# A macaron decoder layer: the mixer run for all 512 tokens at once, its weights split beforehand into DRAM, and one channel group of the long convolution on ScalarE and GpSimd

## The chip, the cores and the metric

The kernel runs on one core of one Trainium2 chip. The time is device microseconds of one execution. PE is TensorE (PEld its weight loads), DVE is VectorE, ACT is ScalarE, POOL is GpSimd, SP is SyncE, which issues most of the DMAs. The span runs from the first to the last instruction of one profiled execution.

## The reference

One layer on x of 512 tokens by 1024, in float32: two half-step SwiGLU FFNs around a token mixer, each behind an RMS norm.

```python
x = x + 0.5 * swiglu(rmsnorm(x, ffn1_norm))          # 1024 -> 2816 -> 1024
h = rmsnorm(x, mix_norm)
c_val, c_gate, r_x, r_gate = split(h @ w_in, 4)      # 512 channels each
u = c_val * sigmoid(c_gate)
u = silu(layernorm(causal_depthwise_conv(u, 31 taps) + bias))
xr = causal_depthwise_conv(r_x, 4 taps) + bias
r = sigmoid(block_diag(xr, w_a) + b_a); i = sigmoid(block_diag(xr, w_x) + b_x)
a = exp(-8 * r * softplus(-lam))
y = scan(h_t = a_t * h_(t-1) + sqrt(1 - a_t^2) * i * xr) * gelu(r_gate)
x = x + concat(u, y) @ w_out                         # 1024 -> 1024
x = x + 0.5 * swiglu(rmsnorm(x, ffn2_norm))
out = rmsnorm(x, final_norm)
```

## The kernel before, in words

**Split products.** Every large product is made of three: a float32 operand is written as hi + lo, hi being the value cast to float32r and lo the difference, and hi*hi, hi*lo and lo*hi are accumulated in PSUM. Weights come in slabs of 128x1024. A slab is loaded by SP into one of 3 `raw` buffers, cast by ACT (L127) and subtracted by DVE or, where a unit is marked shared, by POOL (L141) into one of 5 `hl` buffers. A slab gives 24 matmuls of 512 columns (or 24 of 256 for half of the tokens).

**The list of units.** The kernel is a list `u` of units (L692 on), each one slab's matmuls with what follows them. `run` (L167) walks the list, issues loads, casts and subtractions 5, 3 and 2 slabs ahead, and after each unit steps `chains` (norms, LRU, LayerNorm: generators whose pieces are put between units) and `convs` (single convolution taps, as long as a planner's estimate of DVE's clock lies behind that of PE). A scheduler then orders each engine's instructions once and for all, by priority and by its own estimate of when each is ready; `tc.high_priority(offset=...)` moves a chain's priority, and a higher-priority instruction that isn't ready is passed by others. On the chip each engine follows its fixed order.

**The stages.** First FFN: 22 feature tiles of gate and up, the first 10 with their down projection (`down_a`), the other 12, then `down_b`. `down_b` is run for tokens 0 to 255, then for 256 to 511, because each token block needs two PSUM banks and four are at hand (`pd`; four more are `pp`). Everything from there to the ninth feature tile of the second FFN is done in two halves of 256 tokens, so that one half's chains run beside the other half's matmuls: w_in's 16 slabs are loaded and split twice, as are w_out's 8 and ten of the 12 of `down_b`, and nine FFN2 tiles run as A and, later, B.

**The mixer's chains.** `conv31` (L503) makes 31 taps for each of four channel groups on DVE, `acc = ub * w + acc`, on 128x256 with `acc` in PSUM. `layernorm` (L534) adds the four groups on DVE, averages over channels with a matmul against a matrix of 1/512 (`channel_mean`, L523), subtracts, squares, averages again, and makes u's hi and lo. `rx_units` (L458) evacuate r_x and run the four-tap convolution on DVE with SBUF operands only (L472). `lru` (L568) makes the gates with small float32 matmuls on PE (L577), sigmoid, tanh, exp and square root on ACT, two products on POOL (L581, L600), the scan (L605) and the product with the gelu gate on DVE, then y's hi and lo. `out_units` (L414) waits for u and y of one half. The norms (`norm_chain`, L264) take a square on ACT, two tiny POOL instructions, a scale on DVE (L235), transposes on PE (L251) and an evacuation into `h_hi` and `h_lo`.

Of the kernel before, what the change touches and what calls it, by code (L numbers as in the profile page):

```python
# [21 lines left out]
NG = 7  # L22
NG2A = 9
ND = 4
# [5 lines left out]
POOL_CUT = 1  # L30
POOL_AHEAD = 1.0
DVE_AHEAD = 0.0
NY1 = 0
NY2 = 1
NY3 = 0
NY4 = 0
KEEP = 2
NARROW = 16
PIN_T = True
PIN_A = False  # L40
PR_NORM = 800
PR_CONV = -50
PR_LRU0 = 0
PR_LRU1 = 0
PR_LN = 200
G_ZC = True
G_Y0 = True
YF0 = False
YF1 = True
ORDER = 0  # L50
PR_FIRST = 50
RMS_EPS = 1e-6
LN_EPS = 1e-5

(P_DW, P_DWB, P_LNG, P_LNB, P_LW, P_LCB, P_BA, P_BX, P_LAM, P_N) = (
    0, 31, 32, 33, 34, 38, 39, 40, 41, 42)


@with_exitstack
def layer_kernel(ctx: ExitStack, tc, x, gains, w_g1, w_u1, w_d1a, w_d1b, w_in,  # L60
# [7 lines left out]
    pd = ctx.enter_context(tc.tile_pool(name="pd", bufs=4, space=bass.MemoryType.PSUM))  # L68
    pp = ctx.enter_context(tc.tile_pool(name="pp", bufs=4, space=bass.MemoryType.PSUM))
# [7 lines left out]
    def const(shape, name, dt=F32):  # L77
        return cp.tile(shape, dt, name=name, tag=name)

# [14 lines left out]
    hlast = const([P, 4], "hlast")  # L94
# [11 lines left out]

    clock = {"pe": 0.0, "dve": 0.0, "pool": 0.0}
    chains, convs, done = [], [], {}
# [3 lines left out]


    class Narrow:
        def __init__(self, ap):
            self.ap = ap


    def slab_load(st, src):
        st["raw"] = wp.tile([P, D], F32, name=nm("raw"), tag="raw", bufs=RAW_BUFS)  # L120
        nc.sync.dma_start(st["raw"], src)

    def slab_hi(st, narrow):
        hl = wp.tile([P, 2 * D + 64], F32R, name=nm("hl"), tag="hl", bufs=HL_BUFS)
        o = NARROW if narrow else 0
        st["hl"] = hl[:, o:o + 2 * D].rearrange("p (s d) -> p s d", s=2)
        S.copy(st["hl"][:, 0, :], st["raw"])  # L127

    def slab_lo(st, shared):
        eng = V  # L130
        if shared:
            clock["pool"] = max(clock["pool"], clock["pe"])
            if clock["pool"] - clock["pe"] < POOL_AHEAD:
                eng = G
                clock["pool"] += 2.4
        if eng is V:
            dve(1.15)
        n = POOL_CUT if eng is G else 1
        for i in range(n):
            sl = slice(i * D // n, (i + 1) * D // n)  # L140
            eng.tensor_sub(st["hl"][:, 1, sl], st["raw"][:, sl],  # L141
                           st["hl"][:, 0, sl].bitcast(F32))
# [24 lines left out]
    def run(units, held):  # L167
# [4 lines left out]
        for i, (src, shared, us, mm, evac) in enumerate(x[:5] for x in units):  # L172
# [21 lines left out]
            if evac is not None:  # L194
                evac()
# [644 lines left out]
```

## Time and profile before

| | |
|---|---|
| runs | 936.29, 937.52, 939.07 us; median 937.52 |
| profiled execution | 936.05 us, its span 934.3 us, granted clock 0.982 |
| PE busy | 896.5 us of the span, 96% |
| DVE, ACT, POOL busy | 473.4, 368.7, 211.6 us |
| DMA | 115.94 MB, mean 124 GB/s; nearly all loads issued by SP, 512 KB each |

How to read the rows of the views: a row of the timeline gives start, duration, engine, line, operation, output<-inputs, shapes and count, and in brackets the idle time before it with what ended it. A row of the chain of waits gives start, the share of time on the chain and the instruction. A row of the groups gives line, engine, operation, tiles, shapes, count, then busy time and mean nanoseconds of one, then idle time before the group and what ended it. Overlapping instructions of one engine are merged, so a row's time can be shorter than count by mean.

### The profile page before, as it was taken

Reading aid. Unit: us, or ns where it says so; the run is one execution under the profiler, and the core shown is the slowest. Engines: PE = TensorE matmul, PEld = TensorE weight load, DVE = VectorE, ACT = ScalarE, POOL = GpSimd, SP = SyncE. Lnnn points to the kernel's source line nnn. Section 1 sums busy time; section 2 is a strip of 40 time slices with the busy share of each in tenths; the row PEclk is TensorE's granted clock in tenths of the full one; section 3 lists DMA queues with packets and bytes.
Section 4 is the critical chain, followed back from the end, with each engine's and each line's share of the span. In section 5 each row is a group of like instructions: output and inputs, shape, how many; then the busy total and the mean of one; then the engine's idle time right before and its main releaser. Section 6 shows DMA issues by size and latency. Waiting matters only on the chain.

```text
span 934.3 us, 11886 instructions
## 1 busy us (share of the span) xinstructions
PE 896.5 (96%) x4796; PEld 775.7 (83%) x4796; DVE 473.4 (51%) x677; ACT 368.7 (39%) x502; POOL 211.6 (23%) x120
## 2 busy tenths in 40 slices
PE   8999999999999999979889798999999999999997
PEld 6988888888888889879868797799988888888885
DVE  6533333333333433999999897455523333333224
ACT  6522321222232344357876644644421232223113
POOL 2000000000000058884756895700000000000001
PEclk9999999999999999998989898999999999999999
DMA  7323223222322445553433454455532322232202
GB/s 269 130 93 111 90 91 112 91 91 93 110 91 94 155 135 180 182 186 108 141 132 132 137 186 154 136 169 192 182 113 91 109 94 91 94 110 90 93 21 90
DMA packets 33401, 115.94 MB, mean 124 GB/s; under 512 B 4673, under 2 KB 4801, under 8 KB 33346
## 3 DMA queue, kind: packets, MB, share of 16 engines
q1 hardware_dynamic: 32770, 114.14, 36.9%
q10 hardware_dynamic: 576, 1.05, 0.3%
q8 instruction: 37, 0.61, 0.3%
q14 instruction: 18, 0.15, 0.1%
HBM read 113.07 MB, written 2.10 MB: 123 GB/s over the span
## 4 chain that ended last, share of the span: by engine, by line
PE 83%; DVE 12%; DMA 2%; ACT 1%; issue 1%; POOL 1%; SPq 0%; POOLq 0%; ACTq 0%; DVEq 0%
PE pgate L203 24%; PE pup L203 24%; PE pd L341 8%; PE pd L339 8%; PE pd L340 8%; PE pz L203 6%; DVE pc L516 4%; DVE xr L472 2%; PE pdl L341 1%; PE pdl L340 1%; PE pdl L339 1%; PE ptr L251 1%; DVE xn L235 1%; DMA raw<-in_w_u 1%; POOL hl L141 1%
## 5 line engine op out<-in xcount | busy, mean ns | idle before, releaser
L127 ACT CAST hl<-raw 128x1024 fp32r<-128x1024 f32 x208 | 217.8, 1048 | 327.5 <-PE pup L203 141.6
L141 DVE TENSOR_TENSOR hl<-raw,hl 128x1024 fp32r<-128x1024 f32 x136 | 168.1, 1237 | 283.9 <-ACT hl L127 283.9
L141 POOL TENSOR_TENSOR hl<-raw,hl 128x1024 fp32r<-128x1024 f32 x72 | 181.6, 2530 | 382.7 <-ACT hl L127 381.6
L203 PE MATMUL pup<-h_hi,hl 128*128 128x512 f32 (+1 forms) x880 | 179.7, 346 | 1.1 <-DVE sg L312 1.1
L203 PE MATMUL pgate<-h_hi,hl 128*128 128x512 f32 (+1 forms) x880 | 180.0, 347 | 0.7 <-ACT h_hi L255 0.7
L203 PEld LDWEIGHTS pgate<-h_hi,hl 128*128 128x128 f32 x880 | 144.2, 190 | 21.9 <-ACT h_hi L255 1.4
L203 PEld LDWEIGHTS pup<-h_hi,hl 128*128 128x128 f32 x880 | 144.1, 189 | 21.9 <-DVE sg L312 1.3
L339 PE MATMUL pd<-hl,act 128*128 128x512 f32 x304 | 118.5, 390 | 0.0
L340 PE MATMUL pd<-hl,act 128*128 128x512 f32 x304 | 118.3, 389 | 0.0
L341 PE MATMUL pd<-hl,act 128*128 128x512 f32 x304 | 118.3, 389 | 0.0
L516 DVE SCALAR_TENSOR_TENSOR pc<-ub,ch,pc 128x256 f32<-128x256 f32 x232 | 94.7, 478 | 0.0
L203 PE MATMUL pgate<-h_lo,hl 128*128 128x512 f32 (+1 forms) x440 | 89.8, 346 | 0.0
L203 PE MATMUL pup<-h_lo,hl 128*128 128x512 f32 (+1 forms) x440 | 89.3, 345 | 0.0
L298 ACT ACTIVATE sg<-pgate 128x512 f32<-128x512 f32 (+1 forms) x55 | 28.2, 513 | 151.2 <-PE pgate L203 151.2
L203 PEld LDWEIGHTS pgate<-h_lo,hl 128*128 128x128 f32 x440 | 72.0, 189 | 10.3
L203 PEld LDWEIGHTS pup<-h_lo,hl 128*128 128x128 f32 x440 | 71.7, 188 | 10.2
L312 DVE TENSOR_TENSOR sg<-pup,sg 128x512 f32<-128x512 f32 (+1 forms) x55 | 32.1, 583 | 87.9 <-PE pup L203 87.9
L768 POOL TENSOR_SCALAR sf<-sf 128x1 f32<-128x1 f32 x4 | 1.2, 302 | 319.1 <-ACT sqo L765 319.1
L203 PE MATMUL pz<-h_hi,hl 128*128 128x256 f32 x512 | 70.0, 287 | 0.1
L341 PEld LDWEIGHTS pd<-hl,act 128*128 128x128 f32 x304 | 57.1, 188 | 11.8
L340 PEld LDWEIGHTS pd<-hl,act 128*128 128x128 f32 x304 | 57.1, 188 | 11.8
L339 PEld LDWEIGHTS pd<-hl,act 128*128 128x128 f32 x304 | 57.1, 188 | 11.6
(118 smaller groups left out, 764.7 us busy)
## 6 DMA issues: line engine op xcount, KB each, us to landing
raw<-in_w_g SPq DMA_DIRECT2D x53, 512.0 KB, 3.3
raw<-in_w_u SPq DMA_DIRECT2D x53, 512.0 KB, 3.3
raw<-in_w_in SPq DMA_DIRECT2D x32, 512.0 KB, 3.4
raw<-in_w_d1b SPq DMA_DIRECT2D x22, 512.0 KB, 3.3
raw<-in_w_out SPq DMA_DIRECT2D x16, 512.0 KB, 3.3
raw<-in_w_d2b SPq DMA_DIRECT2D x12, 512.0 KB, 3.2
raw<-in_w_d1a SPq DMA_DIRECT2D x10, 512.0 KB, 3.3
raw<-in_w_d2a SPq DMA_DIRECT2D x10, 512.0 KB, 3.3
```

Of the source, the lines that this page charges most:

```text
L127: S.copy(st["hl"][:, 0, :], st["raw"])
L141: eng.tensor_sub(st["hl"][:, 1, sl], st["raw"][:, sl], st["hl"][:, 0, sl].bitcast(F32))
L203: PE.matmul(ps, w[:, a, k, :], h[:, k, t0:t0 + n], start=(s == 0 and k == 0), stop=(s == 2 and k == KT - 1))
L235: V.scalar_tensor_tensor(out=xn, in0=xt[t], scalar=ss[:, 1:2], in1=g, op0=ALU.mult, op1=ALU.mult)
L251: ins = PE.transpose(pt[:, k, :], xs[0][:, (hf * 4 + k) * P:(hf * 4 + k + 1) * P], ident)
L298: S.activation(sg[:, :n], pg[:, :n], AF.Silu)
L312: V.tensor_mul(sg[:, :n], pu[:, :n], sg[:, :n])
L339: PE.matmul(ps, ahi, whi, start=first, stop=False)
L340: PE.matmul(ps, ahi, wlo, start=False, stop=False)
L341: PE.matmul(ps, alo, whi, start=False, stop=last)
L472: V.scalar_tensor_tensor(out=xr[:, c, :], in0=rxb[:, c, half * HT + k:half * HT + k + HT], scalar=par(c, P_LW + k), in1=xr[:, c, :], op0=A ...
L516: V.scalar_tensor_tensor(out=cv[:, c, :] if j == 30 else acc, in0=src, scalar=par(c, P_DW + j), in1=acc, op0=ALU.mult, op1=ALU.add)
```

## The change

- **One pass.** The mixer runs for all 512 tokens: each w_in and w_out slab is used once. `down_b` runs its first 8 slabs for all four token blocks (8 PSUM banks, now one pool `pb`), and holds its last 4 slabs for two passes of two blocks each. The first two channel groups of the gated convolution input still run as halves A and B; so do the first two feature tiles of both FFNs; all else in FFN2 runs on 512 tokens.
- **Split beforehand.** `split_ahead` loads each of the 24 mixer slabs during the first FFN, casts it on ACT, subtracts on DVE and stores hi and lo to DRAM by DMAs issued on POOL. In the mixer a slab is one 1 MB load straight into `hl` (three of w_out's into six slots of the `act` tag). POOL makes no subtractions any more, in FFN2 either.
- **Convolution.** Three channel groups run on DVE with 31 taps of 128x512 each; the first one has its products made by ACT and its sums, two taps at a time, by POOL.
- **Around it.** The channel sums are four accumulating float32 matmuls instead of DVE sums and one matmul. The four-tap convolution accumulates in PSUM. `hlast` is gone. The output projection makes y's part for token blocks 0 to 2, then, behind the variance, for block 3, then u's part for all four; the norm before FFN2 is started by single token blocks. The yields that held one half's chains behind the other's are gone.

```diff
-    pd = ctx.enter_context(tc.tile_pool(name="pd", bufs=4, space=bass.MemoryType.PSUM))
-    pp = ctx.enter_context(tc.tile_pool(name="pp", bufs=4, space=bass.MemoryType.PSUM))
+    pb = ctx.enter_context(tc.tile_pool(name="pb", bufs=8, space=bass.MemoryType.PSUM))
+    dp = ctx.enter_context(tc.tile_pool(name="dp", bufs=1, space=bass.MemoryType.DRAM))
...
+        while pool_convs and clock["pool"] < clock["pe"]:
+            clock["pool"] = max(clock["pool"], clock["pe"] - 3.0)
+            with tc.high_priority(offset=PR_CONV):
+                us = next(pool_convs[0], None)
+            if us is None:
+                pool_convs.pop(0)
+            else:
+                clock["pool"] += us
...
+    def slab_load(s):
+        if s.split is None:
+            s.raw = wp.tile([P, D], F32, name=nm("raw"), tag="raw", bufs=RAW_BUFS)
+            nc.sync.dma_start(s.raw, s.src)
+    def slab_hi(s):
+        if s.in_act:
+            s.hi, s.lo = slot([P, D], "whi", F32R), slot([P, D], "wlo", F32R)
+        else:
+            hl = wp.tile([P, 2, D], F32R, name=nm("hl"), tag="hl", bufs=HL_BUFS)
+            s.hi, s.lo = hl[:, 0, :], hl[:, 1, :]
+        if s.split is None:
+            S.copy(s.hi, s.raw)
+        elif s.in_act:
+            nc.sync.dma_start(s.hi.bitcast(F32), s.split[:, 0, :])
+            nc.sync.dma_start(s.lo.bitcast(F32), s.split[:, 1, :])
+        else:
+            nc.sync.dma_start(hl.bitcast(F32), s.split)
+    def slab_lo(s):
+        if s.split is None:
+            V.tensor_sub(s.lo, s.raw, s.hi.bitcast(F32))
+            dve(1.15)
...
+            if u.us:
+                step()
+                for g in sides[:1]:
+                    with tc.high_priority(offset=PR_SIDE):
+                        if next(g, None) is None:
+                            sides.remove(g)
...
+    def split_ahead(srcs, kept):
+        for src, dst in zip(srcs, kept):
+            raw, hi, lo = slot([P, D], "sraw"), slot([P, D], "shi", F32R), slot([P, D], "slo", F32R)
+            nc.sync.dma_start(raw, src)
+            yield 1
+            S.copy(hi, raw)
+            V.tensor_sub(lo, raw, hi.bitcast(F32))
+            G.dma_start(dst[:, 0, :], hi.bitcast(F32))
+            G.dma_start(dst[:, 1, :], lo.bitcast(F32))
...
+    def down_b_units(wd, acts, after):
         box = {}
+        def part(k, s, ts):
+            if k == 0:
+                for t in ts:
+                    box[t] = [bank("pd") for _ in range(2)]
+            for t in ts:
                 for oh in range(2):
+                    mm_tok(box[t][oh], acts[k][:, 0, toks(t)], acts[k][:, 1, toks(t)],
+                           s.hi[:, cols(oh)], s.lo[:, cols(oh)], k == 0, k == NB - 1)
...
+        slabs = [Slab(wd[k]) for k in range(NB)]
+        out_ = [Unit([s], 5.44, lambda k=k, s=s: part(k, s, (0, 1, 2, 3)))
+                for k, s in enumerate(slabs[:NB - 4])]
+        for ts in ((0, 1), (2, 3)):
+            for k in range(NB - 4, NB):
+                out_.append(Unit([slabs[k]], 2.72,
+                                 lambda k=k, ts=ts: part(k, slabs[k], ts),
+                                 (lambda ts=ts: fin(ts)) if k == NB - 1 else None))
...
+    def zc_units(c, parts):
+        sgt, sv = Slab(split=ws_in[4 + c]), Slab(split=ws_in[c])
+        box = {}
...
+        def val_out(t0, n):
+            V.tensor_mul(ub[:, c, 30 + t0:30 + t0 + n], box["v"][:, :n], box["s"][:, :n])
+            dve(0.7)
+            if t0 + n == T:
+                if c == 0:
+                    pool_convs.append(conv_pool(c))
+                else:
+                    convs.append(conv_dve(c))
...
+    def channel_sum(key, c, v):
+        if key not in pm:
+            pm[key] = [bank("pm"), 0]
+        ps, n = pm[key]
+        PE.matmul(ps, ones, v, start=n == 0, stop=n == 3)
+        pm[key][1] += 1
+    def conv_done(c):
+        channel_sum("mean", c, conv_out(c))
+        if pm["mean"][1] == 4:
+            chains.append((PR_LN, layernorm()))
+    def conv_dve(c):
+        acc, o = bank("pc"), conv_out(c)
+        for j in range(TAPS):
+            src = ub[:, c, j:j + T]
+            if j == 0:
+                V.tensor_scalar(out=acc, in0=src, scalar1=par(c, P_DW),
+                                scalar2=par(c, P_DWB), op0=ALU.mult, op1=ALU.add)
+            else:
+                V.scalar_tensor_tensor(out=o if j == TAPS - 1 else acc, in0=src,
+                                       scalar=par(c, P_DW + j), in1=acc,
+                                       op0=ALU.mult, op1=ALU.add)
+            yield 0.69
+        conv_done(c)
+    def conv_pool(c):
+        acc, o = slot([P, 2, T], "ca"), conv_out(c)
+        for j in range(0, TAPS, 2):
+            n = min(2, TAPS - j)
+            to = acc if j == 0 else slot([P, 2, T], "cm")
+            for i in range(n):
+                src = ub[:, c, j + i:j + i + T]
+                if j + i == 0:
+                    S.activation(to[:, i, :], src, AF.Identity, scale=par(c, P_DW),
+                                 bias=par(c, P_DWB))
+                else:
+                    S.activation(to[:, i, :], src, AF.Copy, scale=par(c, P_DW + j + i))
+            if j:
+                G.tensor_add(acc[:, :n, :], acc[:, :n, :], to[:, :n, :])
+                yield 1.25 * n
+        G.tensor_add(o, acc[:, 0, :], acc[:, 1, :])
+        yield 1.25
+        conv_done(c)
+    def layernorm():
+        mu = pm["mean"][0]
+        sq = {}
+        yield 1
+        for c in range(4):
+            v = conv_out(c)
+            V.tensor_sub(v, v, mu)
+            dve(0.69)
+            if c % 2 == 0:
+                sq[c // 2] = slot([P, 2, T], "sq")
+            s = sq[c // 2][:, c % 2, :]
+            S.activation(s, v, AF.Square)
+            channel_sum("var", c, s)
+        yield 1
+        rs = sp.tile([P, T], F32, name=nm("rs"), tag="sg", bufs=2)
+        S.activation(rs, pm["var"][0], AF.Sqrt, bias=lneps)
+        V.reciprocal(rs, rs)
+        dve(3.5)
+        done["var"] = True
+        yield 1
+        hi, lo = two("uhi", F32R), two("ulo", F32R)
+        for c in range(4):
+            v, at = conv_out(c), (c // 2, c % 2)
+            V.tensor_mul(v, v, rs)
+            S.activation(v, v, AF.Silu, scale=par(c, P_LNG), bias=par(c, P_LNB))
+            S.copy(hi[at[0]][:, at[1], :], v)
+            V.tensor_sub(lo[at[0]][:, at[1], :], v, hi[at[0]][:, at[1], :].bitcast(F32))
+            dve(1.2)
+        done["u"] = (hi, lo)
...
+        def evac(c):
+            pz, acc = lr[c], bank("px")
+            S.activation(acc, pz, AF.Identity, scale=par(c, P_LW + 3), bias=par(c, P_LCB))
+            S.copy(rxb[:, c, 3:3 + T], pz)
+            for k in range(3):
+                V.scalar_tensor_tensor(out=lr["xr"][c // 2][:, c % 2, :] if k == 2 else acc,
+                                       in0=rxb[:, c, k:k + T], scalar=par(c, P_LW + k),
+                                       in1=acc, op0=ALU.mult, op1=ALU.add)
+                dve(0.69)
...
+    def lru():
+        xr, r, i_, th = lr["xr"], two("r"), two("i"), two("th")
+        for c in range(4):
+            at = (slice(None), c % 2, slice(None))
+            for gi, (to, b) in enumerate(((r, P_BA), (i_, P_BX))):
+                pga = bank("pga")
+                PE.matmul(pga, bd[:, gi, c, :], xr[c // 2][at], start=True, stop=True)
+                S.activation(to[c // 2][at], pga, AF.Sigmoid, bias=par(c, b))
...
+        for q in range(2):
+            G.tensor_mul(xr[q], xr[q], i_[q])
+            clock["pool"] += 2.4
+        for c in range(4):
+            at = (slice(None), c % 2, slice(None))
+            S.activation(th[c // 2][at], r[c // 2][at], AF.Tanh, scale=psp[:, c:c + 1])
+            S.activation(r[c // 2][at], r[c // 2][at], AF.Exp, scale=nsp[:, c:c + 1])
+            if c % 2:
+                yield 1
+        for q in range(2):
+            S.activation(i_[q], r[q], AF.Square)
+            V.scalar_tensor_tensor(out=th[q], in0=i_[q], scalar=1.0, in1=th[q],
+                                   op0=ALU.add, op1=ALU.mult)
+            dve(1.2)
         yield 1
+        for q in range(2):
+            S.activation(th[q], th[q], AF.Sqrt)
+            G.tensor_mul(xr[q], xr[q], th[q])
+            clock["pool"] += 2.4
         yield 1
         for c in range(4):
+            at = (slice(None), c % 2, slice(None))
+            V.tensor_tensor_scan(th[c // 2][at], r[c // 2][at], xr[c // 2][at],
+                                 0.0, ALU.mult, ALU.add)
+            dve(3.5)
             if c % 2:
                 yield 1
+        while "gl" not in done:
             yield 1
+        hi, lo = two("yhi", F32R), two("ylo", F32R)
+        for q in range(2):
+            V.tensor_mul(th[q], th[q], lr["gl"][q])
+            S.copy(hi[q], th[q])
+            V.tensor_sub(lo[q], th[q], hi[q].bitcast(F32))
+            dve(2.4)
+        done["y"] = (hi, lo)
...
+    def out_units(after):
+        sy = [Slab(split=ws_out[4 + c]) for c in range(4)]
+        su = [Slab(split=ws_out[c], in_act=c > 0) for c in range(4)]
+        box = {}
+        def part(t, slabs, key, first, halves=(0, 1)):
+            hi, lo = need(key)
+            if first:
+                box[t] = [bank("po") for _ in range(2)]
+            for oh in halves:
+                for c in range(4):
+                    at = (slice(None), c % 2, toks(t))
+                    mm_tok(box[t][oh], hi[c // 2][at], lo[c // 2][at],
+                           slabs[c].hi[:, cols(oh)], slabs[c].lo[:, cols(oh)],
+                           first and c == 0, not first and c == 3)
...
+        out_ = [Unit(sy, 5.44, lambda t=t: part(t, sy, "y", True)) for t in range(3)]
+        out_ += [Unit([], 0.0, lambda: need("var"))]
+        out_ += [Unit(sy, 5.44, lambda: part(3, sy, "y", True))]
+        out_ += [Unit(su, 2.72, lambda t=t, oh=oh: part(t, su, "u", False, (oh,)),
+                      lambda t=t, oh=oh: fin(t, oh)) for t in range(4) for oh in range(2)]
...
+    u += do(lambda: sides.append(split_ahead(
+        [w_in[i] for i in range(16)] + [w_out[i] for i in range(8)], ws_in + ws_out)))
...
+    u += down_b_units(w_d1b, b1, then(2))
+    z0, z1 = zc_units(0, [A, B]), zc_units(1, [A, B])
+    u += wait("h20") + z0[:2] + z1[:2] + wait("h21") + z0[2:] + z1[2:] + do(gain3)
+    u += zc_units(2, [ALL])
+    u += rx_units() + zc_units(3, [ALL]) + rg_units()
+    u += out_units(lambda t: chains.append(
+        (PR_NORM, norm_chain((t,), gains_of[3], f"h3{t // 2}" if t % 2 else None))))
     u += wait("h30")
+    u += early_units(a2, w_g2, w_u2, wait("h31"))
```

More of the change, by code (lines that the diff above doesn't have):

```diff
@@ L107, in layer_kernel @@
     clock = {"pe": 0.0, "dve": 0.0, "pool": 0.0}
-    chains, convs, done = [], [], {}
+    chains, convs, pool_convs, sides, done = [], [], [], [], {}
     def dve(us):
         clock["dve"] = max(clock["dve"], clock["pe"] - 3.0) + us
[L114 to L142, printed above, removed]
     def step_chains():
@@ L371, in fin @@
                 add_res(t, oh, box["ps"][t], 0.5)
[L373 to L392 removed]
+        out_ = []
```

595 lines of the change are left out of this document (195 added, 400 removed).

## The prediction

> **What bounds the kernel now.** I read the page's head and its slices first, then the stretches between the stages, then the chain of waits.
>
> ```profile
> span 934.3 us, 11886 instructions
> ...
> PE 896.5 (96%) x4796; PEld 775.7 (83%) x4796; DVE 473.4 (51%) x677; ACT 368.7 (39%) x502; POOL 211.6 (23%) x120
> ...
> PE   8999999999999999979889798999999999999997
> ...
> DVE  6533333333333433999999897455523333333224
> ```
>
> PE is at nine tenths nearly everywhere; the dents lie in slices 18 to 26, where DVE is full. The next view sums the stages (columns: stretch, its length, busy time and count of PE, PEld, DVE, ACT, POOL, granted clock, DMA share, GB/s).
>
> ```profile
> 0.00:38.80 38.80, 33.91 (x229) 30.55 (x230) 25.41 (x52) 24.28 (x36) 6.46 (x20) 1.00 0.60 206
> 38.80:310.80 272.00, 272.00 (x1201) 225.28 (x1200) 92.04 (x98) 72.50 (x90) 0.00 (x0) 1.00 0.30 100
> 310.80:400.00 89.20, 89.20 (x495) 77.92 (x495) 48.75 (x94) 38.78 (x45) 54.62 (x26) 1.00 0.52 167
> 400.00:602.00 202.00, 175.90 (x1179) 161.76 (x1178) 177.33 (x285) 131.88 (x191) 142.95 (x63) 0.92 0.43 144
> 602.00:862.20 260.20, 260.20 (x1411) 226.49 (x1410) 106.01 (x120) 83.66 (x113) 4.06 (x5) 1.00 0.37 123
> ```
>
> Both FFN stages are pure PE. In 400 to 602 (mixer) PE idles 202.0 - 175.9 = 26.1 us and DVE is busy 177 of 202: PE waits for DVE. The clock there is 0.92, so waits also cost speed afterwards. What the work itself costs PE, from the chain of waits:
>
> ```profile
> 305.36 5.44 PE pup L203 x24
> 352.49 0.87 PE ptr L251 x8
> 356.10 22.61 PE pz L203 x192
> ...
> 429.04 0.86 PE pga L577 x4
> 429.90 2.74 PE pz L203 x24
> ...
> 436.25 0.86 PE pga L577 x4
> ...
> 626.31 2.83 PE pgate L203 x24
> ...
> 856.74 5.44 PE pup L203 x24
> ```
>
> A full slab costs 5.44 us, one on 256 tokens 2.74 to 2.83, a token block's transposes 0.87, two fp32 gate matmuls of 256 columns 0.86. From 310.8 (305.36 + 5.44) to 862.2 (856.74 + 5.44) the kernel takes 551.4 us. The work in it: down_b 12 slabs 65.3; w_in 32 half slabs at 2.83 90.6; w_out 8 slabs 43.5; gates 16 x 0.43 = 6.9; means 4 x 0.43 = 1.7; transposes 8 x 0.87 = 7.0; FFN2 36 halves 101.9, one pair 10.9, down_a 54.4, second gate/up part 130.6. Sum 512.8. So 38.6 us are lost: the 26.1 idle, the rest slow clock.
>
> **The change, part by part.** *PE work.* The same stretch becomes: down_b 65.3; w_in as 8 halves 22.6 (row 356.10) and 12 full slabs 65.3; w_out 43.5; gates 8 matmuls of 512 columns at 0.86, 6.9; channel sums now four accumulating matmuls each for mean and variance, 8 x 0.86 = 6.9; transposes 7.0; FFN2 8 halves 22.6, 8 pairs 87.0, 54.4, 130.6. Sum 512.1. The PE work is unchanged; all that can be won is the 38.6. With no wait at all the span is 934.3 - 551.4 + 512.1 = **895.0**.
>
> *Splitting ahead.* In the forms view the casts and subtractions of slabs are:
>
> ```profile
> L127 ACT CAST hl<-raw 128x1024 fp32r<-128x1024 f32 x208 | 217.8, 1048 | 327.5 <-PE pup L203 141.6 <-PE pd L341 121.2 <-PE pdl L341 30.2
> L141 POOL TENSOR_TENSOR hl<-raw,hl 128x1024 fp32r<-128x1024 f32 x72 | 181.6, 2530 | 382.7 <-ACT hl L127 381.6 <-DMA raw<-in_w_d1b 0.7
> L141 DVE TENSOR_TENSOR hl<-raw,hl 128x1024 fp32r<-128x1024 f32 x136 | 168.1, 1237 | 283.9 <-ACT hl L127 283.9
> L516 DVE SCALAR_TENSOR_TENSOR pc<-ub,ch,pc 128x256 f32<-128x256 f32 x232 | 94.7, 478 | 0.0
> ...
> L298 ACT ACTIVATE sg<-pgate 128x512 f32<-128x512 f32 x33 | 19.8, 599 | 130.4 <-PE pgate L203 130.4
> ...
> L551 DVE RECIPROCAL rs<-rs 128x256 f32<-128x256 f32 x2 | 3.5, 1746 | 4.8 <-ACT rs L549 4.8
> ```
>
> 24 slabs x 1.05 = 25 us ACT and 24 x 1.24 = 30 us DVE go into 38.8 to 310.8, where ACT is busy 72.5 and DVE 92.0 of 272: room for both, price 0. Without that room each slab would hold its successor up to 2.3 us, 55 in all. Per slab SP issues one more 512 KB load and POOL, wholly idle there, two 512 KB stores; no POOL-issued DMA stands in this trace. A store's price on POOL lies between nothing and the 2.5 us in which POOL walks the same 1024 columns (L141 POOL); two make 5 of the 10.88 us that a slab has. I take nothing. SP's queue is passed by 24 loads; behind them wait only weight loads that run several slabs ahead. In exchange the mixer loses all its casts, all POOL subtractions and all DVE ones, and reads 1 MB per slab:
>
> ```profile
> raw<-in_w_in SPq DMA_DIRECT2D x32, 512.0 KB, 3.4
> ```
>
> 1 MB lies between 3.4 and 6.8 us. Five buffers let a load start when the fifth slab before it is done; only at the seam (down_b keeps its last four slabs for a second pass) is it tight: z1's last slab starts 3.6 us before the mixer and is wanted 5.7 us after; it fits at 6.8. Price 0, at worst 2.
>
> *The long convolution.* Timelines of POOL and DVE:
>
> ```profile
> 382.67 2.40 POOL L141 TENSOR_TENSOR hl<-raw,hl 128x1024 fp32r<-128x1024 f32 x1 [0.34 <-ACT hl L127]
> ...
> 406.51 5.72 POOL L141 TENSOR_TENSOR hl<-raw,hl 128x1024 fp32r<-128x1024 f32 x2
> ```
>
> ```profile
> 379.16 14.19 DVE L516 SCALAR_TENSOR_TENSOR pc<-ub,ch,pc 128x256 f32<-128x256 f32 x36
> 398.50 2.73 DVE L345 SCALAR_TENSOR_TENSOR xt<-pd,xt 128x512 f32<-128x512 f32 x4 [2.29 <-PE pd L341]
> ...
> 409.91 2.60 DVE L472 SCALAR_TENSOR_TENSOR xr<-rxb,ch,xr 128x256 f32<-128x256 f32 x1
> ```
>
> A tap on 256 columns takes 0.39 (36 in 14.19) with POOL at work all the while; four 512-wide residual adds take 2.73, 0.68 each. A 512 tap, which the trace does not show, lies between 0.67 (on the line from 0.39 at 256 columns to 1.24 at 1024, L141 DVE) and 0.68; I take 0.67. 93 taps make 62.3, against 240 x 0.39 = 94 before. POOL adds 15 pairs at 2.4, 36 us, and ACT multiplies 31 taps at 0.6 (L298's 512 columns), 19 us; both are otherwise little used then, and done by about 440. The row at 409.91 shows what POOL costs DVE: with both inputs in SBUF it ends only after POOL's pair, 2.60 for a size that takes a tap 0.39; the taps, with an input in PSUM, pass. The taps and the short convolution (now accumulated in PSUM) are of the second kind.
>
> *The order on PE, from 377.8* (310.8 + 65.3 + 1.7 transposes). First two channels in halves 24.3 with transposes, to 402.1; third 413.0; r_x 434.8; fourth channel with two gate pairs 449.1; r_gate c0 456.3, c1 463.4 (the fourth gate pair sits behind it), c2 468.9, c3 474.3. Then PE wants y, its second half at 475.7.
>
> *The LRU chain* from 463.4 (rows of the first half, where 128x256 or 128x1024 as named):
>
> ```profile
> 437.60 1.28 ACT L578 ACT_TABLE_LOAD   x1
> 438.90 0.47 ACT L578 ACTIVATE r<-pga,ch 128x256 f32<-128x256 f32 x1
> ...
> 445.01 1.07 ACT L593 ACTIVATE i<-r 128x1024 f32<-128x1024 f32 x1
> ...
> 453.69 2.41 POOL L600 TENSOR_TENSOR xr<-xr,th 128x1024 f32<-128x1024 f32 x1
> ...
> 468.09 2.42 DVE L605 TENSOR_TENSOR_SCAN th<-r,xr 128x256 f32<-128x256 f32 x4
> ...
> 479.45 1.21 DVE L617 TENSOR_TENSOR ylo<-th,yhi 128x1024 fp32r<-128x1024 f32 x1
> ```
>
> Table load and two sigmoids 2.5; tanh, table load, exp 2.5; square 1.1; DVE 1.2; table load and square root 2.4; POOL 2.4; two 512 scans 2.4; product with the gate 1.2; cast 1.05; y_lo 1.2; a Gelu and its table in between 1.9; two more microseconds for handovers and taps already running on DVE. Sum 22. y is there at 485.4; PE waits **9.7**. Below: 18 without Gelu and handovers, 5.7. Above: before, from the end of the last gate pair (436.25 + 0.86) to y_lo (480.6) it took 43.5, a wait of 31; 12 us of that lie between POOL's end at 456.1 and the scans at 468.1, behind slab subtractions and normalisation that are gone here or come later. I take the sum.
>
> A wait costs more than itself:
>
> ```profile
> 414.00:421.00 7.00, 1.02 (x9) 0.81 (x7) 7.00 (x14) 1.87 (x3) 3.57 (x2) 0.88 0.63 218
> 421.00:426.00 5.00, 5.00 (x21) 4.73 (x21) 5.00 (x13) 1.29 (x2) 0.00 (x0) 0.50 0.08 34
> 426.00:437.00 11.00, 11.00 (x86) 10.64 (x86) 9.98 (x24) 10.61 (x18) 4.80 (x2) 1.00 0.35 107
> ```
>
> After 6 us of idling PE runs 5 us at half clock: **2.5** lost. The Trainium skill (TensorE: Matmul & The Clock Gate, Part 1) has half clock until about 3.4 us of sustained work; by it the loss would be 1.7 and the time below 0.8 less. The row decides.
>
> *The convolution chain.* DVE from 402.5: taps 62.3; short convolution 12 x 0.67 = 8.0; two products 1.3; LRU 2.5 + 4.8 + 4.8; sum 83.7, end 486.2, or 488.6 if one scan meets POOL. LayerNorm: mean matmul, four subtractions, square, variance, table and root, reciprocal (1746 ns for 256 columns, L551, so 3.5), scale, silu, cast, subtract, 14: u at 502.6, its last channel, 1.2 of ACT work after each one before, at 506.3. PE reaches u at 485.4 + 2.5 + 20.4 rest of y + 4.3 sums = 512.6. u is 10 us early; no wait. The y pass of the fourth token block also waits, for the two banks of the sums: root done near 496, PE there at 507. Behind PE's y wait stand the rest of the projection and all of FFN2, so it counts in full; behind ACT's taps, if they wait for POOL's buffers, stand the evacuations of r_x, which PE's eight banks cover. The norms at both seams run behind 10.9 us of PE work and need about 6.
>
> **Sum:** 895.0 + 9.7 + 2.5 = 907.2. The profiled run took 936.05, 1.75 more than its span: 909. The runs' median of 937.52 is 1.5 above that; I say **910**.
>
> **Rivals.** *y as late as before.* DVE's fixed order puts taps ahead of scans; for it, the 12 us above; against it, slab work is gone from that queue. Wait 31, and 2.5: span 928.5, time 932. Chance 0.20.
>
> *u late.* If DVE is held by 18 us more (table loads queued ahead, LayerNorm in a bad order, as DVE idled 4.8 us for a root before, L551), PE waits 8 and loses 2.5: span 917.7, time 921. Chance 0.08.
>
> *No wait.* The gate matmuls are placed sooner: 895.0 and the 3.2 us between span and runs, 898. Chance 0.07.
>
> *Slower: the first FFN becomes a matter of DMA.* Its 272 us now move 27.2 MB (100 GB/s); 24 x 1.57 MB more make 64.9 MB, 239 GB/s with stores among loads. The first 38.8 us ran at 206 GB/s; if that is the ceiling for a mix, the stage takes 315 us, 43 more, and the time is 953. It turns the result from 217 GB/s downwards (299 us eats the 27 us gain). Against it: at 206 the engines were only 0.60 busy, and loads alone burst higher, as in this stretch of the first FFN (225 to 262):
>
> ```profile
> GB/s 0 0 151 399 18 0 0 0 58 270 257 0 0 0 239 328 0 0 0 0 106 394 66 0 0 53 301 213 0 0 0 0 164 350 53 0 0 93 297 177
> ```
>
> For it: no store of this size is in the trace. Chance 0.10.
>
> **How the numbers follow.** Forecast 0.55, its own range 903 to 919 (y wait 5.7 to 18). The range over cases: from the no-wait case at 898 to the late-y case at 932. A difference under 0.3% (2.8 us) can't be told from no change. Faster takes the forecast, u late, no wait and most of y late: 0.86; same 0.04 from y late with a little more; slower 0.10.
>
> **What would show it.** Right: PE whole and clock 1.00 from 38.8 to 311; no slab casts in the mixer; one PE wait of about 10 us, released by DVE's y, near 475 to 485; DVE idle nowhere between 403 and 486; slice clock low only after that wait; the last gate/up slab ending near 835. Wrong: PE waiting on hl or raw before 311 (the DMA rival), PE waiting on u, DVE taps over 0.68, xr or th instructions stretched to 2.4 beside POOL's adds, or waits of PE for banks held by taps.

## The result, and the profile after

The changed kernel takes **941.69 us** (median of 8 runs, 940.09 to 942.97) against 936.38 us (8 runs, 931.83 to 939.07): a ratio of 1.0059, interval 1.0038 to 1.0081. It is slower by 0.6%, where 910 us were forecast. The profiled execution took 940.52 us.

The head of the changed kernel's page, and its stages (columns as in the prediction's table):

```profile
span 938.3 us, 10242 instructions
```

```profile
38.80:310.80 272.00, 272.00 (x1202) 225.30 (x1200) 120.01 (x121) 96.60 (x114) 24.46 (x46) 1.00 0.64 235
310.80:400.00 89.20, 89.20 (x495) 77.98 (x494) 27.10 (x32) 22.83 (x35) 4.70 (x8) 1.00 0.39 135
400.00:602.00 202.00, 169.62 (x790) 135.03 (x790) 135.40 (x169) 85.72 (x122) 49.70 (x28) 0.91 0.33 115
602.00:865.70 263.70, 263.70 (x1165) 218.44 (x1164) 88.96 (x95) 69.53 (x86) 0.00 (x0) 1.00 0.29 98
```

Every stage but the mixer is as forecast: PE is whole, at full clock. In the mixer PE idles 202.0 - 169.6 = 32.4 us, more than the 26.1 of before, although DVE has much less to do (135 us busy against 177). The span is the forecast's floor of 895.0 plus 43.3. Of these, 32.4 are idling and 8.5 are slow clock behind it (PE's busy time, in stretches of 1 us, times what the granted clock lacks to 1); 2.4 are left over. PE's waits in the mixer:

```profile
PE po L336 <- ACT yhi L610: 17.1, 1, 17.1
PE pm L452 <- DVE cv L468: 9.1, 1, 9.1
PE po L336 <- ACT uhi L519: 3.4, 1, 3.4
PE pm L452 <- ACT sq L505: 1.5, 1, 1.5
```

The first is the wait for y that the forecast had at 9.7. The other three belong to u, where the forecast had none. DVE's timeline shows why both chains are late:

```profile
461.47 4.71 DVE L468 SCALAR_TENSOR_TENSOR pc<-ub,ch,pc 128x512 f32<-128x512 f32 x6
471.55 1.23 DVE L589 SCALAR_TENSOR_TENSOR th<-i,th 128x1024 f32<-128x1024 f32 x1 [5.37 <-ACT i L588]
483.97 2.58 DVE L589 SCALAR_TENSOR_TENSOR th<-i,th 128x1024 f32<-128x1024 f32 x1 [11.20 <-ACT i L588]
486.48 2.33 DVE L600 TENSOR_TENSOR_SCAN th<-r,xr 128x512 f32<-128x512 f32 x2
488.84 3.18 DVE L609 TENSOR_TENSOR th<-th,gl 128x1024 f32<-128x1024 f32 x1
...
497.64 1.23 DVE L611 TENSOR_TENSOR ylo<-th,yhi 128x1024 fp32r<-128x1024 f32 x1 [1.11 <-ACT yhi L610]
498.78 0.74 DVE L468 SCALAR_TENSOR_TENSOR cv<-ub,ch,pc 128x512 f32<-128x512 f32 x1
499.56 0.81 DVE L465 TENSOR_SCALAR pc<-ub,ch 128x512 f32<-128x512 f32 x1
500.41 22.92 DVE L468 SCALAR_TENSOR_TENSOR pc<-ub,ch,pc 128x512 f32<-128x512 f32 x29
```

DVE waits 5.4 and 11.2 us for ACT, with the last tap of channel 2 and all 31 of channel 3 (whose input had been there since about 449) behind the waiting instruction in its list. They come after y, and end at 524.1 instead of 486 to 489. And ACT, for which DVE waits, does this:

```profile
457.13 0.69 ACT L576 ACTIVATE r<-pga,ch 128x512 f32<-128x512 f32 x1 [6.59 <-PE pga L575]
457.99 0.69 ACT L576 ACTIVATE i<-pga,ch 128x512 f32<-128x512 f32 x1 [0.17 <-PE pga L575]
458.69 1.28 ACT L559 ACT_TABLE_LOAD   x1
459.99 0.60 ACT L559 ACTIVATE gl<-pz 128x512 f32<-128x512 f32 x1
460.48 1.33 ACT L583 ACTIVATE th<-r,psp 128x512 f32<-128x512 f32 x2
461.82 1.28 ACT L584 ACT_TABLE_LOAD   x1
463.12 0.72 ACT L584 ACTIVATE r<-r,nsp 128x512 f32<-128x512 f32 x1
463.86 1.28 ACT L559 ACT_TABLE_LOAD   x1
465.15 0.60 ACT L559 ACTIVATE gl<-pz 128x512 f32<-128x512 f32 x1
465.77 1.28 ACT L576 ACT_TABLE_LOAD   x1
467.06 0.69 ACT L576 ACTIVATE r<-pga,ch 128x512 f32<-128x512 f32 x1
```

The four gate pairs come 8 to 10 us apart (440.9, 449.0, 457.1, 467.1). The first three wait for PE, which makes one pair per unit; between the third and the fourth stand Gelus, Tanhs and an Exp of other channels. From 458.7 to 482 ACT loads ten tables of 1.28 us. PE's own product for the last pair:

```profile
463.23 1.88 PE L575 MATMUL pga<-xr,bd 128*128 128x512 f32 x4
```

Two theories follow, and both can be true. **ORDER**: channel 3's taps stand in the wrong place. **LATENCY**: the LRU's chain, on ACT above all, is drawn out. Their common rival is **BOUND**: DVE has too little time, whatever the order.

### The profile page after: what moved, and what is told of

It is laid out like the page before. It is cut to its first block, busy times and chain, and to the rows that moved or that the text cites. A ratio compares the mean times of both kernels' runs of the same rounds, so it can differ in the third digit from the quotient of the medians.

```text
span 938.3 us, 10242 instructions
## 1 busy us (share of the span) xinstructions
PE 893.9 (95%) x4164; PEld 741.1 (79%) x4164; DVE 422.2 (45%) x500; ACT 317.9 (34%) x421; POOL 90.1 (10%) x112
## 4 chain that ended last, share of the span: by engine, by line
PE 90%; DVE 4%; ACT 4%; DMA 1%; issue 1%; SPq 0%; POOL 0%; POOLq 0%; ACTq 0%
PE pgate L236 26%; PE pup L236 26%; PE pz L236 8%; PE pd L338 6%; PE pd L337 6%; PE pd L336 6%; DVE pc L468 2%; PE pdl L337 2%; PE pdl L336 2%; PE pdl L338 2%; PE pm L452 1%; PE ptr L269 1%; PE po L336 1%; PE po L337 1%; PE po L338 1%; DMA raw<-in_w_u 1%
## 5 line engine op out<-in xcount | busy, mean ns | idle before, releaser
L174 DVE TENSOR_TENSOR hl<-raw,hl 128x1024 fp32r<-128x1024 f32 x132 | 161.5, 1225 | 267.4 <-ACT hl L165 267.4
L165 ACT CAST hl<-raw 128x1024 fp32r<-128x1024 f32 x132 | 138.2, 1048 | 291.4 <-PE pup L236 149.3
L236 PEld LDWEIGHTS pgate<-h_hi,hl 128*128 128x128 f32 x768 | 137.0, 189 | 26.0 <-ACT h_hi L274 1.2
L236 PEld LDWEIGHTS pup<-h_hi,hl 128*128 128x128 f32 x768 | 137.0, 189 | 24.9
L336 PE MATMUL pd<-hl,act 128*128 128x512 f32 x256 | 99.8, 390 | 0.0
L338 PE MATMUL pd<-hl,act 128*128 128x512 f32 x256 | 99.6, 389 | 0.0
L337 PE MATMUL pd<-hl,act 128*128 128x512 f32 x256 | 99.6, 389 | 0.0
L236 PEld LDWEIGHTS pup<-h_lo,hl 128*128 128x128 f32 x384 | 68.4, 188 | 12.5
L468 DVE SCALAR_TENSOR_TENSOR pc<-ub,ch,pc 128x512 f32<-128x512 f32 x87 | 65.7, 755 | 2.8
L236 PE MATMUL pz<-h_hi,hl 128*128 128x512 f32 (+1 forms) x320 | 65.8, 354 | 0.0
L236 PEld LDWEIGHTS pz<-h_hi,hl 128*128 128x128 f32 x320 | 52.1, 189 | 9.6 <-issue 2.4
L337 PEld LDWEIGHTS pd<-hl,act 128*128 128x128 f32 x256 | 48.1, 188 | 10.0
L338 PEld LDWEIGHTS pd<-hl,act 128*128 128x128 f32 x256 | 48.1, 188 | 9.9
L336 PEld LDWEIGHTS pd<-hl,act 128*128 128x128 f32 x256 | 48.1, 188 | 9.9
L225 DVE TENSOR_TENSOR slo<-sraw,shi 128x1024 fp32r<-128x1024 f32 x24 | 29.4, 1225 | 22.8 <-ACT shi L224 22.8
```

What stands on the lines that cost most here:

```text
L165: S.copy(s.hi, s.raw)
L174: V.tensor_sub(s.lo, s.raw, s.hi.bitcast(F32))
L225: V.tensor_sub(lo, raw, hi.bitcast(F32))
L236: PE.matmul(ps, w[:, k, :], h[:, k, t0:t0 + n], start=(i == 0 and k == 0), stop=(i == 2 and k == KT - 1))
L336: PE.matmul(ps, ahi, whi, start=first, stop=False)
L337: PE.matmul(ps, ahi, wlo, start=False, stop=False)
```

## The experiments

A ratio is the run against the kernel before on the same chip, with its 95% interval. "u" is the start of the first product with u on PE.

### Channel 3's taps forward

```diff
-        while convs and clock["dve"] < clock["pe"]:
+        while convs and clock["dve"] < clock["pe"] + 10.0:
```

> Only the planner's bound on the convolution is changed: VectorE's taps may be written down while its planned clock is up to 10 us ahead of TensorE's (before: not ahead at all). Everything computed stays. Theory ORDER: the changed kernel loses its gain because channel 3's 31 taps are written down behind the LRU, and VectorE, which goes through its list in order, sits idle (11.2 us in 472.8 to 484.0) in front of LRU instructions while those taps are ready behind them. Then the taps fill that idle time: the last tap ends near 500 instead of 524.1, u is ready near 520 instead of 542.5, y comes 2 to 8 us later than 497.6, and TensorE starts on u at 522 to 527: 922 to 928 us. Rival BOUND: VectorE has too little time in this stage whatever the order; the taps push the LRU's own instructions back by as much as they come forward themselves, y lands near 520, and the time stays at 937 to 943. Rival LATENCY (the ScalarE chain of the LRU with its table loads sets everything): y is as late as now, only the 9.1 us wait for the channel mean goes: 932 to 934.

932.03 us (0.9952, 0.9938 to 0.9966), 9.7 less than the changed kernel. The taps did move, and the last ended at 503.6; u came at 537.1. That is less than ORDER said. It is LATENCY's figure, but not by LATENCY's account: y did not stay where it was, its first product came at 514.3 instead of 493.2. PE's waits tell why:

```profile
PE pm L452 <- DVE cv L468: 22.2, 2, 12.5
```

PE's queue now holds the sums for the channel mean (`pm`) ahead of other work: 9.7 us for channel 1's, in the middle of rx, and 12.5 for channel 3's in front of y. A wait taken from DVE's list came back in PE's.

### The LRU earlier, and two accumulators

The next run also moves rx ahead of channel 2:

```diff
-    u += zc_units(2, [ALL])
-    u += rx_units() + zc_units(3, [ALL]) + rg_units()
+    u += rx_units() + zc_units(2, [ALL])
+    u += zc_units(3, [ALL]) + rg_units()
```

> The bound of the planner as in the run with the taps 10 us ahead, and the four products of the recurrence's input (rx) move ahead of those of convolution channel 2, so that the LRU can begin 11 us of TensorE time earlier. Nothing else. Theory ORDER with LATENCY: the LRU's chain then ends before the last gate's Gelu, y is ready near 484 to 487, the wait for y falls from 17.1 to under 10, and u, which now ends last, is ready near 520 to 523: 918 to 923 us. Theory ORDER alone: u sets the end in both, and the time is the same as with the taps 10 us ahead, within 2 us. Rival BOUND: channel 2's and channel 3's inputs come later, VectorE starves first and is overfull later, u near 535: 934 to 938.

930.71 us (0.9938, 0.9918 to 0.9958): what "ORDER alone" said, but not for its reason. The wait for y is 1.0 us; PE loses 25.6 us at three `pm` sums instead.

Two accumulators, on the changed kernel and on the run just shown:

```diff
-        acc, o = bank("pc"), conv_out(c)
+        accs, o = [bank("pc"), bank("pc")], conv_out(c)
...
+            src, acc = ub[:, c, j:j + T], accs[j % 2]
...
+        V.tensor_add(o, o, accs[1])
```

> Each of VectorE's three channels is summed into two accumulators in turn (even and odd taps) and the two are added at the end: 32 instructions instead of 31, no other edit. Theory DEPENDENT TAPS: a tap that reads the accumulator which the tap just ahead of it wrote takes 0.79 us, one that does not takes 0.66. Then the mean of a tap falls to 0.66 to 0.68 and channel 3, which stands alone in front of u, takes 21 to 22 us instead of 24.5: 938 to 939 us. Rival RATE: the tap's price is its 512 columns and its PSUM operand, whoever wrote it: 0.76 to 0.79 stays, one instruction more per channel, 942 to 943.

> The run before this one (taps 10 us ahead, rx ahead of channel 2) and two accumulators for each channel. DEPENDENT TAPS: 8 to 9 us less VectorE time in front of u, so u near 512 to 515, 910 to 915 us. RATE: the same time as without the two accumulators, or 2 us more. If the two channels' taps already alternate in the run before this one, they no longer depend on each other there either, and the gain is only that of the stretch where one channel stands alone: 1 to 4 us.

On the changed kernel: 941.87 us (1.0066, 1.0047 to 1.0086), no difference. For channel 3, which stands in front of u, it did not test what it was made for:

```profile
500.85 11.05 DVE L470 SCALAR_TENSOR_TENSOR pc<-ub,ch,pc 128x512 f32<-128x512 f32 x14
511.93 0.75 DVE L470 SCALAR_TENSOR_TENSOR cv<-ub,ch,pc 128x512 f32<-128x512 f32 x1
512.71 0.76 DVE L468 TENSOR_SCALAR pc<-ub,ch 128x512 f32<-128x512 f32 x1
513.50 11.04 DVE L470 SCALAR_TENSOR_TENSOR pc<-ub,ch,pc 128x512 f32<-128x512 f32 x14
```

The scheduler put all even taps of channel 3 ahead of all odd ones, so each still follows the tap that it depends on: 11.05 / 14 = 0.79 us. In channels 1 and 2 they did alternate (21 taps in 13.91 us, 0.66 each), but what DVE saved there became waiting for ACT: 8.8 us in front of the first LRU instruction instead of 5.4. On the other run they alternated too:

```profile
463.00 11.94 DVE L470 SCALAR_TENSOR_TENSOR pc<-ub,ch,pc 128x512 f32<-128x512 f32 x18
```

11.94 / 18 = 0.66 us. So DEPENDENT TAPS is right about the price of a tap. But that run took 938.95 us (1.0026, 1.0013 to 1.0038), 8 us more than without: DVE's and PE's lists came out otherwise, y later (waits of 10.2 and 6.1 us) and the mean's sums behind it. No theory had that; which of the new tiles turned the order was not pursued.

### The mean behind y

Taps 10 us ahead, and the four `pm` sums queued behind the third token block's y. The two `cv` tiles get a tag of their own; `conv_out` had also taken a new tile from `act` at every call, used or not; that is gone, and `act` has 17 buffers instead of 19. These edits were not tried one by one.

```diff
-        return cv.setdefault(c // 2, slot([P, 2, T], "cv"))[:, c % 2, :]
+        if c // 2 not in cv:
+            cv[c // 2] = sp.tile([P, 2, T], F32, name=nm("cv"), tag="cv", bufs=2)
+        return cv[c // 2][:, c % 2, :]
...
+        while "y012" not in done:
+            yield 1
+        with tc.issue_after(done["y012"].ins):
+            for c in range(4):
+                channel_sum("mean", c, conv_out(c))
```

> Taps up to 10 us ahead, as in the first run, and two edits: the four sums for the channel mean (pm) are queued on TensorE behind the third token tile's y products instead of as each channel's convolution ends, and the convolution's two output tiles get a tag of their own, so that they no longer take turns with the LRU's tiles. Theory PE QUEUE: in the run with the taps ahead TensorE lost 22.2 us at two pm sums that stood in its queue in front of work that was ready (9.7 at 429.4, 12.5 at 503.6). Without them the products of the last gates end 9 us earlier, and so do the LRU and y: 920 to 925 us. Rival Y LATE: the wait of 12.5 only stood in place of a wait for y, which came at 514; y comes earlier by at most the 9.7, and half of that is eaten by the mean, which now comes later: 927 to 932.

927.29 us (0.9902, 0.9879 to 0.9925): the rival, Y LATE. PE waits no longer for a channel mean, but 15.2 us for y. What is left is ACT.

### The gates together

```diff
                 S.activation(to[c // 2][at], pga, AF.Sigmoid, bias=par(c, b))
-            yield 1
```

On top of the run before, and alone on the changed kernel:

> The run before this one, and the LRU's eight gate products are written down at once and not one channel for each TensorE unit. ScalarE's list then has the eight Sigmoids together, then Tanh and Exp, then Sqrt, then the four Gelus: 3 table loads of 1.28 us where there were 10 or more. Theory LATENCY: the LRU's ScalarE chain (33 us from the last gate pair to y in the changed kernel) falls to 15 to 20 us and ends before the last Gelu, y is ready near 482 to 486, right behind the last gate product, and the convolution's end (near 500) sets the rest: 910 to 918 us. Rival BOUND: VectorE's taps keep the scans and the products behind them back, y near 500 all the same: 920 to 925, as without the edit.

> The changed kernel with one edit alone: the LRU's eight gate products are written down at once. The planner's bound on the taps, the place of the mean and the tags are those of the changed kernel, so channel 3's taps still stand behind y. Theory LATENCY FIRST: the LRU's chain was most of the loss; y is ready near 482, channel 3's taps run from there to 506, the mean comes near 507 (TensorE waits about 10 us for it) and u near 525 instead of 542.5: 922 to 928 us. Theory ORDER FIRST: the place of channel 3's taps was most of it, and with them behind y the time falls by less than the 9.7 us that the taps ahead brought: 932 to 938.

On top: 919.80 us (0.9824, 0.9800 to 0.9849). Alone: **928.51** us (0.9930, 0.9907 to 0.9953), 13.2 less than the changed kernel from one line, half a microsecond above LATENCY FIRST's range and below ORDER FIRST's. Its interval overlaps that of the taps alone (9.7), so which of the two weighs more is not shown. PE and ACT in the run with this edit alone:

```profile
439.20 7.03 PE L575 MATMUL pga<-xr,bd 128*128 128x512 f32 x16
```

```profile
446.38 0.69 ACT L576 ACTIVATE i<-pga,ch 128x512 f32<-128x512 f32 x1
447.08 1.28 ACT L583 ACT_TABLE_LOAD   x1
...
454.90 1.28 ACT L593 ACT_TABLE_LOAD   x1
456.20 2.01 ACT L593 ACTIVATE th<-th 128x1024 f32<-128x1024 f32 x2
458.23 1.28 ACT L559 ACT_TABLE_LOAD   x1
...
475.25 0.60 ACT L559 ACTIVATE gl<-pz 128x512 f32<-128x512 f32 x1 [4.84 <-PE pz L236]
475.74 1.04 ACT L609 CAST yhi<-th 128x1024 fp32r<-128x1024 f32 x1
481.80 1.04 ACT L609 CAST yhi<-th 128x1024 fp32r<-128x1024 f32 x1 [5.02 <-DVE th L608]
```

All gates are through at 447.1, the square roots at 458.2, with two table loads between and a third for the Gelus. The line does two things: it puts the table sets together, and it brings PE's last gate product forward by 19 us, from 465.1 to 446.2. The runs don't tell their shares apart. The last Gelu, which PE's own last product releases, is now what the first half of y waits for; the order of table sets is a rule of the Trainium skill too (ScalarE: Activation LUTs, Table sets: the hidden batching unit): do all calls of one set before the next. These rows agree, and show that a generator's `yield` had decided it.

DVE still has taps in y's way. Here the product for y's second half stands behind twelve of channel 2 and comes at 480.6, so that PE waits 6.0 us for ylo:

```profile
471.18 9.46 DVE L468 SCALAR_TENSOR_TENSOR pc<-ub,ch,pc 128x512 f32<-128x512 f32 x12
```

Channel 3's taps follow y in that run. In the combined one they don't, and there the split of y stood behind some of them:

```profile
477.81 4.71 DVE L472 SCALAR_TENSOR_TENSOR pc<-ub,ch,pc 128x512 f32<-128x512 f32 x6
482.43 2.35 DVE L619 TENSOR_TENSOR ylo<-th,yhi 128x1024 fp32r<-128x1024 f32 x2
```

PE waited 7.4 us for it, with 1.6 for yhi. That run's time lies between the two figures expected.

With rx ahead of channel 2 as well:

> The run before this one with rx ahead of channel 2. LATENCY says y gains nothing any more (the last Gelu sets it), while channel 2's input comes 11 us later and VectorE stands idle meanwhile: 3 to 8 us longer than with channel 2 first. If the LRU's chain still sets y, it is 3 to 6 us shorter.

926.85 us (0.9900, 0.9879 to 0.9921), 7 more, as LATENCY said: DVE starves for 7.6 us before 441.1, and channel 3 ends at 507.9 instead of 493.4.

### Channel 3's last taps behind y

```diff
+                while c == 3 and j >= 11 and "y" not in done:
+                    yield 0
...
+                if c == 3 and j == 11:
+                    tc.keep_in_program_order(ins)
```

> The run with the gates together (919.8 us), and channel 3's taps from the twelfth on stand behind the LRU's last VectorE instruction. Theory ORDER: there the split of y stood behind 6 taps and a scaling behind 8 (ylo at 482.4, although yhi's second half began at 477.9), and TensorE waited 7.4 + 1.6 us in front of y, while the convolution ended at 493.4 and its mean was only summed behind y's third tile near 502. So y comes 5 to 7 us earlier, the convolution's end is the same within 1.5 us, the mean is summed near 495 and u moves from 520.3 to 512 to 515: 912 to 915 us. Rival BOUND: what y gains the convolution loses, u stays near 520: 919 to 921.

**913.11 us** (0.9737, 0.9706 to 0.9768): ORDER again, and the fastest of all. The mixer, DVE and PE's largest waits of this run:

```profile
400.00:602.00 202.00, 192.22 (x926) 156.36 (x925) 139.43 (x179) 87.38 (x130) 48.92 (x28) 0.98 0.37 133
```

```profile
478.10 2.42 DVE L625 TENSOR_TENSOR ylo<-th,yhi 128x1024 fp32r<-128x1024 f32 x2
480.44 15.00 DVE L476 SCALAR_TENSOR_TENSOR pc<-ub,ch,pc 128x512 f32<-128x512 f32 x19
```

```profile
PE po L338 <- ACT uhi L534: 4.3, 1, 4.3
PE po L338 <- ACT yhi L624: 1.6, 1, 1.6
```

PE idles 9.8 us in the mixer instead of 32.4, at clock 0.98; u comes at 514.0. DVE's busy time there is 139 against 135, so BOUND was not what held the changed kernel: the same work on the same engines, in another order, is 28.6 us apart.

### What two parts of the change are worth

w_in split inside the mixer again (only w_out ahead), on the changed kernel and on the run with the gates together; then, on the latter, all four channels of the convolution on DVE:

```diff
-        sgt, sv = Slab(split=ws_in[4 + c]), Slab(split=ws_in[c])
+        sgt, sv = Slab(w_in[4 + c]), Slab(w_in[c])
```

```diff
-                if c == 0:
-                    pool_convs.append(conv_pool(c))
-                else:
-                    convs.append(conv_dve(c))
+                convs.append(conv_dve(c))
```

> The changed kernel, but the sixteen slabs of w_in are loaded and split inside the mixer as before the change; only the eight of w_out are still split during the first FFN. The convolution's share on ScalarE and GpSimd, the order of the work and the whole tokens stay. Theory COVER: the split ahead costs the first FFN nothing, and undoing it gives VectorE 16 x 1.2 us and ScalarE 16 x 1.1 us of work back in 389 to 476, where VectorE is busy 70 of 87 us: channel 2's and 3's taps and the LRU move back by 10 to 19 us, 950 to 960 us. Rival SLACK: VectorE's idle time in 430 to 484 (22 us) takes the splits in, 941 to 945. Rival PRICE: the split ahead costs the first FFN time, the first FFN gets shorter, below 940.

> The run with the gates together (919.8 us), but w_in's sixteen slabs are loaded and split inside the mixer, as in the run where the changed kernel was treated so (945.1 against 941.7: 3.4 us). Theory DVE BOUND: there VectorE's idle time in front of the LRU took the splits; here it has 1.9 us idle in 430 to 480, so the 16 x 1.2 us of splits, less the 12 us idle in 389 to 430, push the convolution's end back by 8 to 15 us: 926 to 934 us. Rival SMALL: the price is 3 to 4 us again, 922 to 924.

> The run with the gates together (919.8 us), but all four channels of the convolution are VectorE's: ScalarE's and GpSimd's quarter is undone. VectorE gets 31 taps of 0.66 to 0.79 us more, 20 to 24 us, GpSimd loses 39 us of additions. Theory DVE BOUND: in that run VectorE is busy 48.1 of the 50 us from 430 to 480, so all of it lands in front of u: convolution end 513 to 517 instead of 493.4, 930 to 936 us. Rival SLACK: VectorE has idle time between 389 and 430 (12.4 us of 41), which takes half of it: 921 to 927. Rival CONTENTION: GpSimd's additions and ScalarE's products hold VectorE's instructions back (2.0 to 2.5 us instead of 1.2 for a scan or a split beside them); without them the other taps get shorter and the quarter is worth under 3 us.

On the changed kernel the split inside the mixer takes 945.13 us (1.0092, 1.0065 to 1.0120), 3.4 more, with intervals that overlap: SLACK, at its edge; DVE's idle time took most of it. (COVER's 70 busy us of 87 are those of the weight loads, in the column beside; DVE was busy 57.6.) On the run in better order it takes 929.09 (0.9904, 0.9866 to 0.9942), 9.3 more, and the convolution all on DVE takes 932.82 (0.9951, 0.9936 to 0.9966), 13.0 more: DVE BOUND both times. The stretch 430 to 480 of the changed kernel, of the run with the gates together, and of these two on top of it:

```profile
430.00:480.00 50.00, 46.03 (x185) 34.28 (x183) 29.86 (x40) 29.30 (x37) 15.29 (x8) 1.00 0.52 186
```

```profile
430.00:480.00 50.00, 44.64 (x182) 33.65 (x180) 48.11 (x62) 26.25 (x36) 19.51 (x10) 0.98 0.55 198
```

```profile
430.00:480.00 50.00, 44.35 (x180) 33.40 (x179) 49.41 (x58) 31.00 (x40) 22.52 (x11) 0.99 0.52 184
```

```profile
430.00:480.00 50.00, 47.09 (x193) 35.67 (x191) 45.42 (x62) 27.31 (x35) 10.50 (x4) 1.00 0.52 186
```

DVE is busy 29.9 of 50 us in the first: work taken from it there buys little. In the second it is busy 48.1, and work put back moves channel 3's end from 493.4 to 509.8 and 515.0. Of these 16.4 and 21.6 us, 9.3 and 13.0 reach the time: DVE's wait for the channel mean, which stands behind y on PE, shrinks from 12.0 to 2.2 us in both and takes in part of them. The third part, whole tokens in place of halves, was not undone by itself.

## Why the prediction was wrong, point by point

- *PE work is unchanged, 895.0 without a wait*: right within 2.4 us. The stages outside the mixer show it, and the rest of what was lost is 32.4 of waiting and 8.5 of slow clock.
- *Splitting ahead, price 0 in the first FFN*: right. PE is busy 272.00 of 272.00 at 235 GB/s, so the rival that ended slower fell with its ceiling of 206. The kernel is slower by another road.
- *Loads of 1 MB, no wait*: right; PE is busy 87.0 us of the 87.0 from 389 to 476.
- *POOL done near 440, last gate pair at 463.4*: right, the second within 1.7 us (POOL 440.9, the products of the last pair end at 465.1).
- ***The LRU chain, 22 us***: **the first step that failed.** From the end of the last gate products (463.23 + 1.88) to the end of ylo (498.9) it took 33.8. The sum counted four table loads from there on (one with a Gelu); there are seven, 3.8 us more, with two more Gelus. It took the chain as if ACT and DVE were free when an operand came: instead the last two Sigmoids waited for ACT until 467.1, and Tanh of the first half, whose gates were ready at 441.6 and 449.7, ran at 460.5 behind a Gelu. It noticed DVE's instructions beside POOL (two of them took 2.58 and 3.18 instead of 1.2) for one scan only.
- ***DVE: "sum 83.7, end 486.2", "u is 10 us early; no wait"***: **the second, and the graver in kind.** The sum let DVE work on whatever was ready. Its list has 32 taps behind an LRU instruction that wasn't. The convolution ended some 36 us late, and PE waited 14.0 for u and its two sums (9.1 + 3.4 + 1.5). The rival "y as late as before" had the order the other way ("taps ahead of scans"); the rival "u late" had 18 us on DVE from other causes, and no case had y and u late together.
- *A tap, 0.67*: mis-sized. The 93 taps lasted 0.755 on average, 70 us and not 62: 0.66 holds only where an instruction of another accumulator stands between two taps; alone it is 0.79. Not decisive: the run at 913.11 has the same taps.
- *A wait costs 2.5 more at half clock*: right in kind (the granted clock is 0.50 from 493 to 500); there were four waits, and 8.5 us in all.
- *What would show it wrong*: three of the signs that it named are in the trace: PE waiting on u, taps over 0.68, and `th` stretched beside POOL.

Nothing of this was in the change's own work. With the orders mended the same parts give 913.11. That this lies inside the forecast's own 903 to 919 is partly luck: in that run PE waits 2.3 us for y, where the sum had 9.7, and 5.8 for u and the variance, where it had none. The prediction's price list was nearly right, and its schedule was one that nobody had written: it priced the change under the best order, where the trace of before (12 us between POOL and the scans) already showed lists that wait.

## What to carry to other kernels

Work that is taken off a busy engine is worth its price only if that engine then runs without gaps: 9.3 us for the split in a tight order, 3.4 (not clear of noise) in a loose one. So when a change lets chains that used to alternate run side by side, predict each engine's list in order, with what stands behind every waiting instruction, and not only its sum; and look first at PE's, which small sums of late chains can block. On ACT, gather the pieces of one function before the next, and check how many table loads stand between the first and the last link of the chain that the end waits for.

## What the runs showed of the hardware

- DVE's `acc = ub * w + acc` on 128x512 starts every 0.79 us behind the tap that wrote its accumulator, and every 0.66 us behind another instruction, though each lasts 0.75. The Trainium skill (VectorE: DVE Perf Modes, The DRAIN you can't avoid) says that the next operation doesn't start until the pipe is empty, and that "a next op that is not held starts earlier". The first figure fits the first of these and the second the other: there successive instructions overlap by 0.09.
- A change of table sets costs ACT 1.3 us between two instructions (457.99 + 0.69 to 459.99). The Trainium skill (ScalarE: Activation LUTs, What ACT_TABLE_LOAD costs) states about 1.28 for the load and 1.38 more for a drain; no such gap stands in these rows.
- With GpSimd-issued stores of 512 KB beside the loads the first FFN moves 235 GB/s at a DMA share of 0.64, and PE doesn't notice.
